# A mixture-of-experts block on one Trainium2 core: the router stage splits x itself, and the norm's weight is applied when gathered rows leave PSUM

## The chip, the cores and the metric

The kernel runs on one core of a Trainium2 chip. Its time is the device time of one execution in microseconds (us). Three executions of the kernel before took 1015.25, 1016.13 and 1021.9 us; the median is 1016.13 us. Engines are named as in the profile: PE (TensorE; PEld is its weight load), DVE (VectorE), ACT (ScalarE), POOL (GpSimd) and SP, which here only issues DMAs.

## What is computed

Two transformer blocks run on 256 tokens of width 1024. The change lies in the last third of the first block, the mixture of experts. After the memory attention `x` is updated by a projection with `w_o_mem`, and then:

```
h   = x * rsqrt(mean(x*x) + eps) * norm_ffn          # rms_norm
pg  = softmax(h @ w_rg + b_rg);  group = argmax(pg)
pe  = softmax((h @ w_re + b_re)[group]);  two best of 8 experts
y   = sum over both: weight * ((silu(h @ w_gate[e]) * (h @ w_up[e])) @ w_down[e])
x   = x + y
```

There are 32 experts, each with three matrices of 1024 x 512 float32 (6 MB), and all of them are read from HBM. A second block follows (attention and a squared-relu MLP).

## The kernel before, in words

**Stages.** `first_mixers` ends with the memory attention. `moe` then adds the projection `w_o_mem` to `x` in two halves of 512 columns (chunks `c` and `last`), routes the tokens (class `Router`), gathers each expert's tokens into slots of 64 rows, runs 16 pairs of experts (`pair(p)`), and scatters the results back into four PSUM accumulators. `second` follows.

**Two parts.** Where float32 exactness matters, an operand is split in a high part (rounded to fp32r by ACT) and a low part (the difference, by DVE or POOL), and both are multiplied. The gather uses that: `hh` and `hl` (`R.h`) are the high and low part of the normed tokens, and a one-hot matrix `D` of each group of four experts selects rows by matmul (line 1043: 4 matmuls for each of 8 slices of 128 features, 32 for a group `q` of four experts, 8 groups). The result leaves PSUM at lines 1047 (DVE) and 1049 (ACT), 512 columns at a time, into `XG[q]`.

**The router stage** (lines 1110 to 1161) is written out by hand: the order of the calls is the order of the instructions on PE, ACT, DVE and POOL. For each half of the tokens (`tb` 0 and 1):

- `project`, `add` (line 1089): `x` gets its last columns, and ACT sums the squares (line 233).
- `transposed` (785 to 790) and `logits` (795): `x`, not normed, is transposed and multiplied by the router's weights, into which `gains` (779) has put the norm's weight.
- `rms` (243 and 69 to 87, nine small DVE instructions) gives the token's factor `r`.
- `gained` (1095): POOL writes `y = x * gain`, a scaled copy of `x`, in the feature order of the gather. It lives in one of the two `raw2` buffers; the weight's rows fill one of the two `gb` buffers.
- The two parts: for `tb` 0 ACT makes `hh = y * r` (1123) and DVE `hl` (1124); for `tb` 1 ACT scales `y` (1142), rounds it to `hh` (1143), and POOL subtracts (1144).
- `groups` (800 to 805) scales the logits and finds the best group.

After both halves come `experts` (815 to 831, DVE), `counts` (838 to 840, PE), `slots`, `one_hots` (1025, 1026), `gather(0)` and then the first pair's matmuls (1062). `keep_warm` (1100) issues products of the identity that nobody reads; `init` (1104) puts `x` into the accumulators, after which x's own buffer is free for weights.

**Weights.** `feed` (991) issues the experts' loads on SP's queue, 1 MB each, in the order of use. A load goes to the next place of the list `HOMES` (r: six `raw` buffers, w: the split buffers `whi` and `wlo`, h, g: the two `gb` buffers, 2: `raw2`, x: the buffer of `x`), and only if that place is counted free in `space`; `freed` hands a place back. SP's own order is set by a scheduler, in which a load is put where its buffer is expected to come free; SP issues in that order and waits at each for the buffer's last reader.

Of the kernel before, what the change touches and what calls it, by code (L numbers as in the profile page):

```python
# [9 lines left out]
F32 = mybir.dt.float32  # L10
# [4 lines left out]
AF = mybir.ActivationFunctionType  # L15
OP = mybir.AluOpType
# [152 lines left out]
def tok(tb):  # L169
    return slice(tb * 128, tb * 128 + 128)  # L170


def half(n):
    return slice(n * 512, n * 512 + 512)
# [42 lines left out]
def load_gain(k, name, queue=None):  # L217
    gb = k.pa.tile([128, 1024], F32, name="gb", bufs=2)
    src = k.I[name]
    (queue or k.nc.gpsimd).dma_start(gb, bcast_rows(src, 1024))  # L220
    return gb
# [15 lines left out]
def rms(k, parts):  # L237

    v = small(k, 1, "rv")
    if len(parts) == 1:  # L240
        k.nc.vector.tensor_scalar(v, parts[0], RMS_EPS, None, op0=OP.add)
    else:
        k.nc.vector.tensor_scalar(v, parts[0], parts[1], RMS_EPS, op0=OP.add, op1=OP.add)
    return rsqrt(k, v, 1)
# [691 lines left out]
def moe(k, oT):  # L936
# [4 lines left out]
    x = k.x  # L941
    wg, wu, wd = I["w_gate"][0], I["w_up"][0], I["w_down"][0]
    R = Routing()
    with ExitStack() as ctx:
# [6 lines left out]
        R.flag = mp.tile([1, 1], I32, name="flag")  # L951
        R.raw2 = ctx.enter_context(tc.tile_pool(name="raw2", bufs=RAW2))

        y = R.raw2.tile([128, 2048], F32, name="raw").rearrange("p (t n) -> p t n", t=2)
        route_tables(k, R)
        gain = load_gain(k, "norm_ffn")
        w_o = I["w_o_mem"][0]
        parts = [[], []]
        c = Chunk(k, cols(w_o, 0))
# [18 lines left out]
        order = [(p, kind, h, i) for p in range(NP) for kind in range(3) for h in range(2) for i in range(2)]  # L978
        homes = cycle(HOMES)
        space = {kind: HOMES.count(kind) for kind in HOMES}  # L980
        for kind in "w2xg":
            space[kind] -= SPL if kind == "w" else 1
        weights, ahead = {}, []

# [24 lines left out]
        def freed(kind, n=1):  # L1009
            space[kind] += n  # L1010
            feed()
# [22 lines left out]
        def gather(q, parts):  # L1034

            if q not in XG:
                XG[q] = gathered_tiles(q)
            for j in parts:
                ps = k.wk.tile([128, 2, 256], F32, name="wk")
                for r in range(2):  # L1040
                    terms = [(h, tb) for h in R.h for tb in range(2)]
                    for i, (h, tb) in enumerate(terms):
                        nc.tensor.matmul(ps[:, r], h[:, tb, tok(2 * j + r)], DD[q][:, tb],
                                         start=(i == 0), stop=(i == 3))
                dst = XG[q][j // 2][:, j % 2 * 2:j % 2 * 2 + 2].rearrange("p a e s -> p a (e s)")
                if j % 2:
                    nc.vector.tensor_copy(dst, ps)
                else:
                    nc.scalar.activation(dst, ps, AF.Copy)

        def side(i):

# [36 lines left out]
            nc.vector.tensor_add(xs, xs, acc[tb])  # L1089
            parts[tb].append(mean_sq(k, xs, mp.tile([128, 512], F32, name="usb", bufs=1)))  # L1090

        def gained(tb, n):
            out = y[:, tb].rearrange("t (kt p) -> t p kt", kt=8)[:, n * 64:n * 64 + 64]
            xs, gs = (v[:, half(n)].rearrange("t (p kt) -> t p kt", kt=8) for v in (x[:, tb], gain))
            nc.gpsimd.tensor_tensor(out, xs, gs, op=OP.mult)

        def keep_warm(tb, n):

# [9 lines left out]
        macc = [[], []]  # L1108
        pool = nc.gpsimd
        with tc.manual_schedule(engines=order_of):  # L1110
            gained(0, 0)
            gained(1, 0)
            project(0, UNITS)
            q.transposed(0, 0, nc.scalar)
            add(0)
            gained(0, 1)
            q.transposed(1, 0, nc.vector)
            feed()
            project(1, UNITS[:4])
            q.transposed(0, 1, nc.scalar)  # L1120
            r0 = rms(k, parts[0])
            q.gains()
            nc.scalar.activation(hh[:, 0], y[:, 0], AF.Copy, scale=r0)
            nc.vector.scalar_tensor_tensor(hl[:, 0], y[:, 0], r0, hh[:, 0].bitcast(F32),
                                           op0=OP.mult, op1=OP.subtract)
            project(1, UNITS[4:])
            macc[0].extend(k.acc.tile([128, 512], F32, name="acc") for _ in range(2))
            freed("w", SPL)
            q.logits(0, 0)
            add(1)  # L1130
            q.transposed(1, 1, nc.scalar)
            gained(1, 1)
            freed("g")
            r1 = rms(k, parts[1])
            keep_warm(0, 2)
            q.logits(0, 1)
            keep_warm(0, 2)
            q.logits(1, 0)
            q.groups(0, r0)
            keep_warm(0, 2)  # L1140
            q.logits(1, 1)
            nc.scalar.activation(y[:, 1], y[:, 1], AF.Copy, scale=r1)
            nc.scalar.activation(hh[:, 1], y[:, 1], AF.Copy)
            pool.tensor_tensor(hl[:, 1], y[:, 1], hh[:, 1].bitcast(F32), op=OP.subtract)
            freed("2")
            q.groups(1, r1)
            init(0)
            macc[1].extend(k.acc.tile([128, 512], F32, name="acc") for _ in range(2))
            q.experts()
            keep_warm(1, 3)  # L1150
            q.counts()
            init(1)
            freed("x")
            q.slots()
            one_hots(0)
            q.exps()
            gather(0, (0, 1))
            q.slots_by_group()
            gather(0, (2, 3))
            q.rows()  # L1160
            one_hots(1)
# [147 lines left out]
def spill(k, R, macc):  # L1309

    nc, tc, I = k.nc, k.tc, k.I
    n_over = nc.values_load(R.flag[0:1, 0:1], min_val=0, max_val=512)
    with tc.If(n_over > 0):
        hT = k.pa.tile([128, 8, 256], F32, name="hTl0", bufs=1)
        for kt in range(8):
            ps = k.wk.tile([128, 256], F32, name="wk")
            h = R.mp.tile([128, 2, 128], F32, name="usb", bufs=1)
            nc.vector.tensor_add(h, *(t[:, :, tok(kt)].bitcast(F32) for t in R.h))
            for tb in range(2):
                nc.tensor.transpose(ps[:, tok(tb)], h[:, tb], k.ident)  # L1320
            nc.scalar.activation(hT[:, kt], ps, AF.Copy)
        with tc.For_i(0, NE, 1) as e:

            def half_load(name, j):
                w = R.raw2.tile([128, 2048], F32, name="raw")
                src = I[name][0][ds(e, 1)].rearrange("o (p a) n -> p (o a) n", p=128)
                a, n = src.shape[1:]
                nc.sync.dma_start(w.rearrange("p (a n) -> p a n", n=n), src[:, j * a // 2:(j + 1) * a // 2])
                return w

            pg = [[k.wk.tile([128, 512], F32, name="wk") for _ in range(2)] for _ in range(2)]
            for i, name in enumerate(("w_gate", "w_up")):
                for j in range(2):
                    w = half_load(name, j)
                    for kt in range(4):
                        for tb in range(2):
                            nc.tensor.matmul(pg[tb][i], hT[:, 4 * j + kt, tok(tb)], w[:, half(kt)],
                                             start=(j == 0 and kt == 0), stop=(j == 1 and kt == 3))
            aT = []
            at = [R.mp.tile([128, 4, 128], F32, name=name, bufs=1) for name in ("sg", "v")]  # L1340
            for tb in range(2):
                a = R.mp.tile([128, 512], F32, name=("usb", "gsb")[tb], bufs=1)
                nc.scalar.activation(a, pg[tb][0], AF.Silu)
                nc.vector.tensor_mul(a, a, pg[tb][1])
                pt = k.wk.tile([128, 4, 128], F32, name="wk")
                for f in range(4):
                    nc.tensor.transpose(pt[:, f], a[:, f:512:4], k.ident)
                t = at[tb]
                nc.scalar.activation(t, pt, AF.Copy)
                aT.append(t)  # L1350
            py = [[k.wk.tile([128, 512], F32, name="wk") for _ in range(2)] for _ in range(2)]
            for j in range(2):
                w = half_load("w_down", j)
                for f in range(2):
                    for tb in range(2):
                        for n in range(2):
                            nc.tensor.matmul(py[tb][n], aT[tb][:, 2 * j + f], w[:, half(2 * f + n)],
                                             start=(j == 0 and f == 0), stop=(j == 1 and f == 1))
            for tb in range(2):
                for n in range(2):  # L1360
                    ys = R.mp.tile([128, 512], F32, name=("usb", "gsb")[n], bufs=1)
                    nc.vector.tensor_scalar(ys, py[tb][n], R.wov[:, tb, ds(e, 1)], None, op0=OP.mult)
                    nc.tensor.matmul(macc[tb][n], k.ident, ys, start=False, stop=True,
                                     skip_group_check=True)
# [320 lines left out]
```

## Time and profile before

| | before |
|---|---|
| median of three executions | 1016.13 us (1015.25 to 1021.9) |
| profiled execution | 1020.27 us, span 1018.5 us |
| PE busy | 946.6 us (93%) |
| DVE, ACT, POOL busy | 445.7, 330.2, 137.5 us |
| HBM read | 291.28 MB, 287 GB/s over the span |
| mean granted clock of PE | 0.981 |

Times of rows are microseconds from the start of the span. In the table by stretch a busy time is a sum within the stretch, and PEclk is the share of the full clock that was granted (1.00 is 2.4 GHz, 0.50 is 1.2 GHz). In a timeline a row can stand for several instructions (xN); its length is from the first one's start to the last one's end, and square brackets hold the engine's idle time before it and what ended it.

### The profile page before, as it was taken

To read this page: it belongs to the slowest core of one execution; us is meant where nothing else is said; L and a number is where in the kernel's file an instruction comes from. 1 tells how busy PE (TensorE), PEld (TensorE's weight loads), DVE (VectorE), ACT (ScalarE), POOL (GpSimd) and SP (SyncE) were. 2 spreads that over 40 slices of the span, in tenths; PEclk is the share of its full clock that TensorE was granted. 3 is DMA by queue.
4 is the path that set the end of the run, shared out by engine and by line. 5 is a ranking of instruction groups with operands and counts; after the bars stand their busy time and mean duration, and the time that the engine had idled before them with its cause. 6 is when DMAs were issued, how large, how long until landed. Compare 5 with 4: busy or idle time off the path is not lost. (4 is left out here: it accounts for less than half of the span.)

```text
span 1018.5 us, 13363 instructions
## 1 busy us (share of the span) xinstructions
PE 946.6 (93%) x5308; PEld 658.4 (65%) x5308; DVE 445.7 (44%) x810; ACT 330.2 (32%) x518; POOL 137.5 (13%) x83
## 2 busy tenths in 40 slices
PE   9989999998999999999989999878898979999996
PEld 8969889884344444444434444325888859999995
DVE  6896875644221211121111211106845578444554
ACT  6647554531110111011111101105553436444541
POOL 1231121230000000000000000002313332211220
PEclk9989999999999999999999999998998989999999
DMA  9953553597999999999999999999534435556501
GB/s 356 351 167 133 176 186 125 176 348 268 401 425 421 424 423 422 425 422 424 422 420 423 421 421 425 423 424 352 197 125 125 155 115 169 203 189 189 201 1 42
DMA packets 85712, 293.23 MB, mean 288 GB/s; under 512 B 6992, under 2 KB 15728, under 8 KB 72080
## 3 DMA queue, kind: packets, MB, share of 16 engines
q1 hardware_dynamic: 84752, 289.56, 73.4%
q0 software_dynamic: 896, 2.79, 0.8%
q8 instruction: 43, 0.70, 0.3%
q14 instruction: 21, 0.17, 0.1%
HBM read 291.28 MB, written 1.05 MB: 287 GB/s over the span
## 5 line engine op out<-in xcount | busy, mean ns | idle before, releaser
L131 ACT ACTIVATE whi<-raw 128x1024 fp32r<-128x1024 f32 x156 | 162.9, 1058 | 149.6 <-PE acc L182 60.5
L140 DVE TENSOR_TENSOR wlo<-raw,whi 128x1024 fp32r<-128x1024 f32 x114 | 142.9, 1263 | 105.1 <-ACT whi L131 102.9
L140 POOL TENSOR_TENSOR wlo<-raw,whi 128x1024 fp32r<-128x1024 f32 x42 | 103.0, 2456 | 333.7 <-ACT whi L131 331.2
L180 PE MATMUL acc<-hTh,whi 128*128 128x256 f32 x352 | 102.3, 291 | 0.0
L182 PE MATMUL acc<-hTh,wlo 128*128 128x256 f32 x352 | 101.1, 287 | 0.3 <-DVE wlo L140 0.3
L181 PE MATMUL acc<-hTl,whi 128*128 128x256 f32 x352 | 100.8, 286 | 0.0
L1221 DVE COPY usb<-wk 128x512 f32<-128x512 f32 x16 | 11.0, 690 | 203.3 <-PE wk L1062 185.2
L1062 PE MATMUL wk<-raw,hTh 128*64 128x512 f32 x312 | 88.5, 600 | 10.5 <-DMA raw<-in_w_up 5.0
L1185 PE MATMUL wk<-raw,v 128*64 128x512 f32 x232 | 71.1, 595 | 10.8 <-issue 8.5
L1196 ACT ACTIVATE hTl<-wk,wc 128x512 fp32r<-128x512 f32 x32 | 22.0, 688 | 165.3 <-PE wk L1185 165.3
L180 PEld LDWEIGHTS acc<-hTh,whi 128*128 128x128 f32 x352 | 68.7, 195 | 1.3 <-issue 1.0
L182 PEld LDWEIGHTS acc<-hTh,wlo 128*128 128x128 f32 x352 | 68.5, 195 | 0.5 <-DVE wlo L140 0.5
L181 PEld LDWEIGHTS acc<-hTl,whi 128*128 128x128 f32 x352 | 68.6, 195 | 0.2
L1062 PE MATMUL wk<-raw,hTl 128*64 128x512 f32 x208 | 67.4, 594 | 0.0
L1062 PEld LDWEIGHTS wk<-raw,hTh 128*64 128x64 f32 x312 | 28.3, 138 | 58.5 <-issue 42.3
L181 PE MATMUL acc<-wlo,hTh 128*128 128x512 f32 x160 | 63.8, 399 | 1.7 <-DVE wlo L140 1.7
L1197 DVE SCALAR_TENSOR_TENSOR hTl<-wk,wc,hTl 128x512 fp32r<-128x512 f32 x32 | 24.0, 751 | 91.7 <-ACT hTl L1196 89.9
L180 PE MATMUL acc<-whi,hTh 128*128 128x512 f32 x160 | 63.6, 398 | 0.0
L180 PE MATMUL wk<-hTh,whi 128*128 128x256 f32 x224 | 63.5, 284 | 0.0
L182 PE MATMUL acc<-whi,hTl 128*128 128x512 f32 x160 | 63.5, 398 | 0.0
L182 PE MATMUL wk<-hTh,wlo 128*128 128x256 f32 x224 | 63.4, 283 | 0.0
L181 PE MATMUL wk<-hTl,whi 128*128 128x256 f32 x224 | 63.4, 283 | 0.0
(409 smaller groups left out, 1775.8 us busy)
## 6 DMA issues: line engine op xcount, KB each, us to landing
raw<-in_w_up SPq DMA_DIRECT2D x49, 1024.0 KB, 11.0
raw<-in_w_down SPq DMA_DIRECT2D x45, 1024.0 KB, 11.1
raw<-in_w_gate SPq DMA_DIRECT2D x32, 1024.0 KB, 14.1
whi<-in_w_down SPq DMA_DIRECT2D x25, 512.0 KB, 11.1
wlo<-in_w_down SPq DMA_DIRECT2D x25, 512.0 KB, 9.9
whi<-in_w_up SPq DMA_DIRECT2D x20, 512.0 KB, 12.0
wlo<-in_w_up SPq DMA_DIRECT2D x20, 512.0 KB, 11.4
whi<-in_w_gate SPq DMA_DIRECT2D x19, 512.0 KB, 10.5
```

Source lines behind the costliest of these rows:

```text
L131: self.k.nc.scalar.activation(hi, self.quarter(len(self.his)), AF.Copy)
L140: eng.tensor_tensor(lo, self.quarter(i), self.his[i].bitcast(F32), op=OP.subtract)
L180: nc.tensor.matmul(out, lh, rh, start=start, stop=False, skip_group_check=True)
L181: nc.tensor.matmul(out, lh, rl, start=False, stop=False, skip_group_check=True)
L182: nc.tensor.matmul(out, ll, rh, start=False, stop=stop, skip_group_check=True)
L1062: nc.tensor.matmul(ps[side(i)], xg[:, 2 * (p % 2) + i], w[:, half(kt % 2)], start=(kt == 0), stop=(kt == 7), tile_position=(0, 64 * i), sk ...
L1185: nc.tensor.matmul(py[n][side(i)], v[:, f, side(i)], w[:, half(n)], start=(f == 0), stop=(f == 3), tile_position=(0, 64 * i), skip_group_c ...
L1196: nc.scalar.activation(yh[:, s], py[n], AF.Copy, scale=R.wc[:, p:p + 1])
L1197: nc.vector.scalar_tensor_tensor(yl[:, s], py[n], R.wc[:, p:p + 1], yh[:, s].bitcast(F32), op0=OP.mult, op1=OP.subtract)
L1221: nc.vector.tensor_copy(u, ps)
```

## The change

The scaled copy `y` goes. Both parts are made from `x` itself, for both halves of the tokens with one ACT and one DVE instruction (`normed`), so POOL has no arithmetic left in the stage. The parts lie in x's feature order, so the gather's stationary operand now takes every eighth column (`2 * j + r:1024:8`). The norm's weight, as a table `R.gain` of 8 columns, is multiplied in where a gathered slice leaves PSUM: 256 columns at a time, the even slice by ACT and the odd one by DVE. The six idle products between the logits go; three ahead of `counts` stay. `groups(0)` moves ahead of `rms` of the second half, and the places `2` and `g` are counted free from the start.

```diff
--- before.py
+++ after.py
@@ -951,9 +951,9 @@
         R.flag = mp.tile([1, 1], I32, name="flag")
         R.raw2 = ctx.enter_context(tc.tile_pool(name="raw2", bufs=RAW2))
 
-        y = R.raw2.tile([128, 2048], F32, name="raw").rearrange("p (t n) -> p t n", t=2)
         route_tables(k, R)
-        gain = load_gain(k, "norm_ffn")
+        R.gain = mp.tile([128, 8], F32, name="gain")
+        nc.gpsimd.dma_start(R.gain, I["norm_ffn"].rearrange("o (p kt) -> p (o kt)", kt=8))
         w_o = I["w_o_mem"][0]
         parts = [[], []]
         c = Chunk(k, cols(w_o, 0))
@@ -978,7 +978,7 @@
         order = [(p, kind, h, i) for p in range(NP) for kind in range(3) for h in range(2) for i in range(2)]
         homes = cycle(HOMES)
         space = {kind: HOMES.count(kind) for kind in HOMES}
-        for kind in "w2xg":
+        for kind in "wx":
             space[kind] -= SPL if kind == "w" else 1
         weights, ahead = {}, []
 
@@ -1040,13 +1040,15 @@
                 for r in range(2):
                     terms = [(h, tb) for h in R.h for tb in range(2)]
                     for i, (h, tb) in enumerate(terms):
-                        nc.tensor.matmul(ps[:, r], h[:, tb, tok(2 * j + r)], DD[q][:, tb],
+                        nc.tensor.matmul(ps[:, r], h[:, tb, 2 * j + r:1024:8], DD[q][:, tb],
                                          start=(i == 0), stop=(i == 3))
-                dst = XG[q][j // 2][:, j % 2 * 2:j % 2 * 2 + 2].rearrange("p a e s -> p a (e s)")
-                if j % 2:
-                    nc.vector.tensor_copy(dst, ps)
-                else:
-                    nc.scalar.activation(dst, ps, AF.Copy)
+                for r in range(2):
+                    kt = 2 * j + r
+                    dst = XG[q][j // 2][:, kt % 4].rearrange("p e s -> p (e s)")
+                    if r:
+                        nc.vector.tensor_scalar(dst, ps[:, r], R.gain[:, kt:kt + 1], None, op0=OP.mult)
+                    else:
+                        nc.scalar.activation(dst, ps[:, r], AF.Copy, scale=R.gain[:, kt:kt + 1])
 
         def side(i):
 
@@ -1089,10 +1091,11 @@
             nc.vector.tensor_add(xs, xs, acc[tb])
             parts[tb].append(mean_sq(k, xs, mp.tile([128, 512], F32, name="usb", bufs=1)))
 
-        def gained(tb, n):
-            out = y[:, tb].rearrange("t (kt p) -> t p kt", kt=8)[:, n * 64:n * 64 + 64]
-            xs, gs = (v[:, half(n)].rearrange("t (p kt) -> t p kt", kt=8) for v in (x[:, tb], gain))
-            nc.gpsimd.tensor_tensor(out, xs, gs, op=OP.mult)
+        def normed(tb, r):
+
+            nc.scalar.activation(hh[:, tb], x[:, tb], AF.Copy, scale=r)
+            nc.vector.scalar_tensor_tensor(hl[:, tb], x[:, tb], r, hh[:, tb].bitcast(F32),
+                                           op0=OP.mult, op1=OP.subtract)
 
         def keep_warm(tb, n):
 
@@ -1108,41 +1111,28 @@
         macc = [[], []]
         pool = nc.gpsimd
         with tc.manual_schedule(engines=order_of):
-            gained(0, 0)
-            gained(1, 0)
             project(0, UNITS)
             q.transposed(0, 0, nc.scalar)
             add(0)
-            gained(0, 1)
             q.transposed(1, 0, nc.vector)
             feed()
             project(1, UNITS[:4])
             q.transposed(0, 1, nc.scalar)
             r0 = rms(k, parts[0])
             q.gains()
-            nc.scalar.activation(hh[:, 0], y[:, 0], AF.Copy, scale=r0)
-            nc.vector.scalar_tensor_tensor(hl[:, 0], y[:, 0], r0, hh[:, 0].bitcast(F32),
-                                           op0=OP.mult, op1=OP.subtract)
+            normed(0, r0)
             project(1, UNITS[4:])
             macc[0].extend(k.acc.tile([128, 512], F32, name="acc") for _ in range(2))
             freed("w", SPL)
             q.logits(0, 0)
             add(1)
             q.transposed(1, 1, nc.scalar)
-            gained(1, 1)
-            freed("g")
-            r1 = rms(k, parts[1])
-            keep_warm(0, 2)
             q.logits(0, 1)
-            keep_warm(0, 2)
             q.logits(1, 0)
             q.groups(0, r0)
-            keep_warm(0, 2)
+            r1 = rms(k, parts[1])
             q.logits(1, 1)
-            nc.scalar.activation(y[:, 1], y[:, 1], AF.Copy, scale=r1)
-            nc.scalar.activation(hh[:, 1], y[:, 1], AF.Copy)
-            pool.tensor_tensor(hl[:, 1], y[:, 1], hh[:, 1].bitcast(F32), op=OP.subtract)
-            freed("2")
+            normed(1, r1)
             q.groups(1, r1)
             init(0)
             macc[1].extend(k.acc.tile([128, 512], F32, name="acc") for _ in range(2))
@@ -1315,10 +1305,10 @@
         for kt in range(8):
             ps = k.wk.tile([128, 256], F32, name="wk")
             h = R.mp.tile([128, 2, 128], F32, name="usb", bufs=1)
-            nc.vector.tensor_add(h, *(t[:, :, tok(kt)].bitcast(F32) for t in R.h))
+            nc.vector.tensor_add(h, *(t[:, :, kt:1024:8].bitcast(F32) for t in R.h))
             for tb in range(2):
                 nc.tensor.transpose(ps[:, tok(tb)], h[:, tb], k.ident)
-            nc.scalar.activation(hT[:, kt], ps, AF.Copy)
+            nc.scalar.activation(hT[:, kt], ps, AF.Copy, scale=R.gain[:, kt:kt + 1])
         with tc.For_i(0, NE, 1) as e:
 
             def half_load(name, j):
```

On PE, in the router stage from the first half's logits to the counts (`lp` is the tile of the logits, `ident` the identity, `M` the one-hot of the chosen experts), the one piece of the difference reads:

```order
-L795 MATMUL wk<-wr,hTl_2345 128x36 x4
 L785 MATMUL wk<-ident,x 128x128 x4
-L1100 MATMUL acc<-ident 128x128 x2
-L795 MATMUL wk<-wr,hTl_2345 128x36 x4
-L1104 MATMUL acc<-x,ident 128x512 x2
+L795 MATMUL wk<-wr,hTl_2344 128x36 x12
+L1107 MATMUL acc<-x,ident 128x512 x2
+L1103 MATMUL acc<-ident 128x128 x3
 L838 LDWEIGHTS tri
```

Of the rows that repeat, two more pairs of idle products and two more groups of four logits' products are left out here. Afterwards twelve products of the logits follow one another, then `init(0)` and the three idle products, as before.

On DVE, from the second half's add on, the kernel before has (`gp` and `lg` are the scaled logits; the row L87 ends `rms`):

```order
L1089 TENSOR_TENSOR x<-x,acc 128x512
L243 TENSOR_SCALAR rv<-ms 128x1
L87 TENSOR_SCALAR rqr<-rqt,rqx,rqi 128x1
L800 SCALAR_TENSOR_TENSOR gp<-wk,rqr,rb 128x4
L805 MAX_INDEX gi_2350<-g_2349,gp 128x8
L815 TENSOR_TENSOR g_2572<-iof,gi_2350 128x8
L817 TENSOR_TENSOR ep<-lg,g_2572 128x64
```

and the changed kernel, in the same place (of `rms` the first and the last row, of `groups` the first of each):

```order
L1091 TENSOR_TENSOR x<-x,acc 128x512
L805 MAX_INDEX gi_2349<-g_2348,gp 128x8
L243 TENSOR_SCALAR rv<-ms 128x1
L87 TENSOR_SCALAR rqr<-rqt,rqx,rqi 128x1
L1097 SCALAR_TENSOR_TENSOR hl<-x,rqr,big_2355 128x1024
L802 SCALAR_TENSOR_TENSOR lg<-wk,rqr,rb 128x32
L815 TENSOR_TENSOR g_2560<-iof,gi_2349 128x8
L817 TENSOR_TENSOR ep<-lg,g_2560 128x64
```

`groups(0)` has moved from behind `rms` to ahead of it, and the low part of the second half, POOL's before, stands between `rms` and `groups(1)`.

On SP, at the loads of chunk `last` (`in_w_o_mem`) and the first experts', the difference begins:

```order
-L116 DMA raw<-in_w_o_mem 128x4x512 x4
-L1005 DMA raw<-in_w_gate 128x2048 x2
-L1005 DMA raw<-in_w_up 128x2048
+L116 DMA raw<-in_w_o_mem 128x4x512 x2
 L1005 DMA gb<-in_w_gate 128x1024
```

The first of the two half-size loads to the `gb` buffers now stands ahead of the last two loads of `w_o_mem`. Further on, the second of them and a 1 MB load to `raw2` have moved from behind the loads to `whi` and `wlo` to ahead of them.

## Rows read from the trace of the kernel before

**Rows 1.** Busy table by stretch: length, busy us (count) by engine, clock, DMA share, GB/s

```profile
230.00:237.00 7.00, 4.34 (x17) 1.98 (x16) 6.10 (x27) 0.00 (x0) 2.20 (x1) 1.00 0.86 324
242.00:246.00 4.00, 4.00 (x20) 1.29 (x18) 2.33 (x6) 0.00 (x0) 0.00 (x0) 1.00 0.02 4
300.00:690.00 390.00, 360.64 (x1736) 162.90 (x1734) 64.89 (x114) 41.81 (x66) 2.34 (x1) 1.00 1.02 423
```

**Rows 2.** Timeline of SP's queue, 205 to 262: start, length, instruction

```profile
236.60 0.33 SPq L1005 DMA_DIRECT2D x<-in_w_up  x1
245.47 0.80 SPq L1005 DMA_DIRECT2D raw<-in_w_up  x2
```

**Rows 3.** Timeline of PE, 215 to 262: start, length, instruction [idle before]

```profile
225.37 0.61 PE L1100 MATMUL acc<-ident 128*128 128x128 f32 x4
225.82 0.98 PE L795 MATMUL wk<-wr,hTl 128*128 128x36 f32 x8
...
234.53 0.18 PE L838 MATMUL wk<-M,tri 128*128 128x32 bf16 x1 [2.58 <-DVE M L831]
...
234.60 1.96 PE L1104 MATMUL acc<-x,ident 128*128 128x512 f32 x4
...
237.47 0.36 PE L1043 MATMUL wk<-D,big 128*128 128x256 f32 x1 [0.55 <-DVE d L864]
```

**Rows 4.** Timeline of DVE, 205 to 262

```profile
222.94 1.28 DVE L1124 SCALAR_TENSOR_TENSOR hl<-raw,rqr,big 128x1024 fp32r<-128x1024 f32 x1 [2.00 <-ACT big L1123]
224.15 0.68 DVE L1089 TENSOR_TENSOR x<-x,acc 128x512 f32<-128x512 f32 x1
225.67 0.21 DVE L243 TENSOR_SCALAR rv<-ms 128x1 f32<-128x1 f32 x1 [0.85 <-ACT usb L233]
...
227.31 0.21 DVE L800 SCALAR_TENSOR_TENSOR gp<-wk,rqr,rb 128x4 f32<-128x4 f32 x1
...
229.52 0.22 DVE L800 SCALAR_TENSOR_TENSOR gp<-wk,rqr,rb 128x4 f32<-128x4 f32 x1 [1.49 <-PE wk L795]
...
230.28 1.95 DVE L815 TENSOR_TENSOR g<-iof,gi 128x8 f32<-128x8 f32 x1
232.26 0.22 DVE L817 TENSOR_TENSOR ep<-lg,g 128x64 f32<-128x64 f32 x1
```

**Rows 5.** Timeline of ACT, 205 to 262

```profile
221.76 1.14 ACT L1123 ACTIVATE big<-raw,rqr 128x1024 fp32r<-128x1024 f32 x1
...
227.48 1.15 ACT L1142 ACTIVATE raw<-raw,rqr 128x1024 f32<-128x1024 f32 x1 [1.31 <-DVE rqr L87]
```

**Rows 6.** Timeline of POOL, 180 to 262

```profile
229.86 2.34 POOL L1144 TENSOR_TENSOR hl<-raw,big 128x1024 fp32r<-128x1024 f32 x1 [3.67 <-ACT big L1143]
```

**Rows 7.** Weight loads by line: ns min/median/max, first and last start, form

```profile
L785 PEld LDWEIGHTS wk<-ident,x x16: 138/140/143, 216.8 to 225.2; 128*128 128x128 f32 x16
...
L1043 PEld LDWEIGHTS wk<-D,big x128: 186/188/202, 236.5 to 622.5; 128*128 128x128 f32 x128
...
L1168 PEld LDWEIGHTS wk<-ident,gsb x64: 195/212/220, 257.0 to 681.7; 128*128 128x128 f32 x64
```

**Rows 8.** Timeline of PE, two places where it resumes after a gap

```profile
519.85 1.09 PE L1062 MATMUL wk<-raw,hTh 128*64 128x512 f32 x1 [2.81 <-DVEq L1313]
...
831.23 1.08 PE L1506 MATMUL wk<-ident,a 128*128 128x128 f32 x4 [3.43 <-DVE a L1499]
```

**Rows 9.** Busy table of the stretches in which the clock came back there

```profile
522.00:524.00 2.00, 2.00 (x10) 0.67 (x8) 0.00 (x0) 0.00 (x0) 0.00 (x0) 0.80 1.03 416
836.00:838.00 2.00, 2.00 (x9) 1.59 (x8) 0.82 (x2) 0.00 (x0) 0.00 (x0) 0.80 0.02 4
```

**Rows 10.** Costliest groups: count, busy us, mean ns, idle before and its releasers

```profile
L1062 PE MATMUL wk<-raw,hTh 128*64 128x512 f32 x312 | 88.5, 600 | 10.5 <-DMA raw<-in_w_up 5.0 <-DVEq L1313 2.8 <-DMA raw<-in_w_gate 2.7
```

**Rows 11.** The same view for two copies out of PSUM on DVE

```profile
L1047 DVE COPY hTh<-wk 128x512 f32<-128x512 f32 x8 | 5.5, 692 | 23.5 <-PE wk L1043 23.5
...
L366 DVE TENSOR_TENSOR t<-wk,t 128x256 fp32r<-128x256 f32 x8 | 3.0, 418 | 0.8 <-ACT t L365 0.8
```

## The prediction

> **What bounds the kernel now.** I read the busy table by stretch first. From 300 to 690 us the DMA engines are busy without a break (share 1.02) at 423 GB/s, while PE computes 360.64 of 390 us [rows 1]: the sixteen pairs of experts run at the speed at which weights arrive. The only line of PE in there that waits for data is 1062, with 5.0 + 2.7 = 7.7 us put down to weight loads in the whole run [rows 10]; that is PE's spare time in the loop. So work added or saved inside the loop counts only beyond that.
>
> Second, where does this stream start? From 242 to 246 the DMA share is 0.02 [rows 1]. SP's queue tells why: the load into x's buffer is issued at 236.60, and the next one only at 245.47, when the first pair has used up its first weights [rows 2]. All buffers are full and the stream stands still until PE computes. The amount loaded by then is fixed by the buffers, so **the end moves with the start of the first pair**, one for one, and loading earlier gains nothing.
>
> Third, what sets that start: the chain through the router stage. PE waits 2.58 us for DVE's row 831 before the counts, and 0.55 us for the one-hots [rows 3]. DVE is busy for 6.10 of the 7.00 us from 230 on [rows 1]. The reader should see in DVE's timeline that the comparison of 128x8 numbers at line 815, begun at 230.28, takes 1.95 us, though line 817, with 64 columns, takes 0.22; it ends when POOL's subtraction ends, 229.86 + 2.34 = 232.20 [rows 4, 6]. POOL's work holds DVE up there, on the path.
>
> **The change part by part.** All times are of the profiled execution (1020.27 us with a span of 1018.5; the median of the runs shown, 1016.13, is 4.1 lower); I add the sum to the median.
>
> *DVE's chain.* Up to the second add (224.15) nothing on it moves: `hh` of the first half waited for ACT's copy, not for `y`. Now `groups(0)` comes next and needs the logits of the first half. PE starts them where the first idle products stood, 225.37, and eight records last 0.98: 226.35 [rows 3]. A dependent instruction follows 0.04 after its source (1123 ends at 222.90, 1124 starts at 222.94) [rows 4, 5], so 226.39. `groups` takes 230.28 - 229.52 = 0.76: 227.15. `rms` takes 227.48 - 225.67 = 1.81 until ACT can start on its result [rows 4, 5]: 228.96. ACT's `hh` takes 1.14 as line 1123: 230.10. DVE's `hl` starts 0.04 later and the next instruction 224.15 - 222.94 = 1.21 after that [rows 4, 5]: 231.35. `groups(1)` 0.76: line 815 starts at 232.11. No POOL instruction is left to hold it up, so it takes about as long as line 817, 0.22 [rows 4]; line 817 starts at 232.33, against 232.26 before. **Sum: +0.07 us.** The 1.73 us that the stall gives back are spent on `hl`, which now stands in DVE's line.
>
> *The gather's weight loads.* The stationary operand is read with a step of eight floats. The trace has no such load. Below: a load of 188 ns that hides behind a matmul costs nothing, +0. Above: the transposes with a step of four floats (1168) load in 212 ns, those without a step (785) in 140 [rows 7]; if 72 ns more show in full, 32 loads cost 2.3 us on the path. A gain is excluded, since the same numbers are read from more places. PE overlaps a load with the matmul before, so I take a value nearer to the row of hidden loads: 0.02 each, **+0.7 us**. In the loop there are seven more groups, 224 of the 256 loads [rows 7]: 224 x 0.02 = 4.5 us, under the 7.7 that PE has to spare, so nothing.
>
> A rule that speaks against this change: the Trainium skill, "SBUF — State Buffer", section "Door 1: The DMA port swizzle (why `[64,N]` ≈ `[32,N]`)", says that SBUF is read in lines of 16 bytes, and that an access pattern pays when successive elements fall on different lines, so that float32 may be read with a step of up to four free of charge. Here every element falls on a line of its own. The trace differs for the step of four, which is not free in it; the page gives no price, so by the rule the term of 0.7 is some positive number, and by the row it is bounded by 2.3.
>
> *The idle products.* Three blocks go, each moving what follows by about 225.82 - 225.37 = 0.45 [rows 3], 1.4 in all. PE, which ended at 234.53 - 2.58 = 231.95, ends at about 230.6 and stays idle until 234.60: 4.0 us. They are work for nothing only while the clock stays up. Before, the gap of 2.58 us left it at 1.00 [rows 1, 3]. But after gaps of 2.81 and 3.43 us PE resumed with matmuls of 1.09 and 1.08 us [rows 8], and the clock was at 0.80 in the mean of 522 to 524 and of 836 to 838 [rows 9]. With two levels, 1.2 and 2.4 GHz, a mean of 0.80 over 2 us is 0.8 us at the lower, so it came back at 522.8 and 836.8: 2.9 and 5.6 us after work had resumed. I expect the same here. `init(1)` takes 0.45 a record at full clock (1.96 for four, the last 0.6 of which overlaps) [rows 3], 0.9 at half. If the clock returns 2.9 us after 234.65, three records are done at half speed and the last follows at full: the gather goes on at 237.9 rather than 237.54 (237.47 + 0.07), +0.35. If after 5.6 us, `init(1)` ends at 238.25 and the gather runs 2 us at half: 0.7 + 1.0 = +1.7. I take the middle, **+1.0 us**.
>
> *Copies out of PSUM.* A slice of 256 columns takes DVE 0.42 against 0.69 for 512 [rows 11]. There are twice as many, but ACT and DVE share each tile. Cover: the first pair's first weights need slices 0 to 3, and PE is still gathering slices 4 to 7 then. If the cover went, one copy, 0.4 us, would show. In the loop it is hidden with all else.
>
> *DMAs.* The 512 KB of weight rows become a table of 4 KB, issued last on POOL's queue, well ahead of the gather. Loads to `gb` and `raw2`, 2 MB in all, are issued earlier. One of them now stands ahead of `last`'s chunk on SP's queue. Its buffer's reader is long done; what it costs the chunk is 0.5 MB at 423 GB/s [rows 1], 1.2 us of a wait that the memory attention covers. On the other side nothing is gained, since the stream stands still at 242 either way. x's load follows `init(1)`; it moves by 1.7 us at most, towards a stretch in which the stream stands still for 4.
>
> Sum: 0.07 + 0.7 + 1.0 = **+1.8 us**, 1017.9 us (1022.1 for an execution like the profiled one).
>
> **The rivals.**
>
> *Slower: strided loads bind PE.* If each load shows 72 ns, the path takes 2.3 us, and the loop 224 x 0.072 = 16.1, of which 7.7 are spare and 8.4 are not. With the clock's 1.0 and 0.07 that is +11.8: 1027.9 us. It decides from 7.7 / 224 = 34 ns a load on. For it: line 1168's 212 ns. Against it: PE pulls loads ahead of matmuls of 256 columns, and in the gather before 188 ns stay hidden behind them. Chance 0.08; twice that price (1050) 0.01.
>
> *The clock stays up*, as after the gap of 2.58 us, since three idle products still stand close to the gap: +0.8, 1016.9 us. Chance 0.25.
>
> *The stall stays.* If line 815 is slow for a reason of its own and not for POOL's, `hl` is added and nothing given back: 1.8 + 1.73 = +3.5, 1019.6 us. For it: it is the only instruction of its kind. Against it: its end agrees with POOL's to 0.03 us. Chance 0.08.
>
> *Faster: the loop is bound by PE.* Then the half copy ahead of `v` (0.69 - 0.42 = 0.27 us in each of 14 pairs) would count: -3.8, with the sum 1014.1 us. Against it: DMA share 1.02. Chance 0.06.
>
> **How the numbers follow.** My forecast has a chance of 0.52, with bounds 0.07 + 0.35 + 0 = +0.4 and 0.07 + 1.7 + 2.3 = +4.1, so 1016.5 to 1020.2. Three executions of one kernel spread over 6.6 us, and a median can lie a microsecond or two lower on another day; to take in the PE-bound case and the stall that stays, the range goes from 1014 to 1022. What it leaves out is mostly the strided case. A measurement tells some 1% (10 us) from no change, and only the strided loads reach that: faster 0.01, same 0.90, slower 0.09.
>
> **What would show it.** In the changed kernel's profile the comparison (815) should take about 0.2 us and line 817 start 232.33 - 224.15 = 8.2 us after the second add; `hl` of the second half should stand in front of it with 1.28 us. The granted clock should fall below 1.00 between 230 and 240. The gather's loads should last between 188 and 260 ns, and its matmuls start at most 0.03 us further apart than before. The DMA share should be near zero just ahead of the first pair's second half, for longer than before, and 1.02 from there on. I am wrong if the loop's share falls below 1, if the gather's matmuls start 0.07 us further apart than before, or if the first pair starts more than 4 us later or more than 1 us earlier, counted from the second add.

## The result and the profile after

The changed kernel takes 1062.97 us (median of four executions, 1061.44 to 1068.18), the kernel before 1016.88 beside it (1015.25 to 1021.9): a ratio of 1.0433, with a 95% interval of 1.0403 to 1.0463. It is **46 us slower**; the prediction was 1017.9, in 1014 to 1022. The profiled execution has a span of 1059.4 us against 1018.5, and a mean granted clock of 0.964 against 0.981.

The busy table by stretch, after (length, then busy us and count of PE, PEld, DVE, ACT, POOL, then clock, DMA share, GB/s):

```profile
230.00:237.00 7.00, 3.23 (x14) 1.94 (x13) 5.08 (x29) 1.01 (x1) 0.00 (x0) 0.86 0.59 240
242.00:246.00 4.00, 4.00 (x18) 4.00 (x18) 1.14 (x4) 0.95 (x2) 0.00 (x0) 1.00 0.27 115
300.00:690.00 390.00, 365.50 (x1584) 174.71 (x1586) 67.24 (x126) 43.62 (x74) 0.00 (x0) 0.95 0.97 394
```

Against [rows 1] the loop's DMA share has fallen from 1.02 to 0.97 and its clock from 1.00 to 0.95, and in the same 390 us PE gets through 1584 matmuls where it did 1736. The weights no longer set the pace. From 242 to 246 PEld, the weight load, is busy all of the 4.00 us. The gather's line, by form, says why (ns min/median/max, first and last start):

```profile
L1043 PEld LDWEIGHTS wk<-D,big x128: 312/338/343, 238.3 to 675.4; 128*128 128x128 f32 x128
L1043 PE MATMUL wk<-D,big x128: 397/407/738, 238.3 to 675.6; 128*128 128x256 f32 x128
```

A load with the step of eight floats lasts 338 ns, not 188 [rows 7] (the other half of the loads, those of `hl`, have the same median). The timelines of PE, DVE and ACT show the router stage and one of the waits in the loop (start, length; in brackets the idle time before, and what ended it):

```profile
235.48 0.19 PE L838 MATMUL wk<-M,tri 128*128 128x32 bf16 x1 [3.77 <-DVE M L831]
235.56 3.39 PE L1107 MATMUL acc<-x,ident 128*128 128x512 f32 x4
239.14 0.65 PE L1043 MATMUL wk<-D,hl 128*128 128x256 f32 x2
239.63 0.65 PE L1043 MATMUL wk<-D,big 128*128 128x256 f32 x2
240.11 0.65 PE L1043 MATMUL wk<-D,hl 128*128 128x256 f32 x2
246.93 3.65 PE L1064 MATMUL wk<-raw,hTl 128*64 128x512 f32 x16
...
328.39 0.65 PE L1043 MATMUL wk<-D,hl 128*128 128x256 f32 x2
330.76 1.09 PE L1175 MATMUL wk<-raw,v 128*64 128x512 f32 x1 [1.72 <-issue]
```

```profile
225.25 0.68 DVE L1091 TENSOR_TENSOR x<-x,acc 128x512 f32<-128x512 f32 x1
231.05 1.28 DVE L1097 SCALAR_TENSOR_TENSOR hl<-x,rqr,big 128x1024 fp32r<-128x1024 f32 x1 [1.22 <-ACT big L1096]
233.00 0.17 DVE L815 TENSOR_TENSOR g<-iof,gi 128x8 f32<-128x8 f32 x1
233.21 0.22 DVE L817 TENSOR_TENSOR ep<-lg,g 128x64 f32<-128x64 f32 x1
...
329.58 0.48 DVE L1049 TENSOR_SCALAR hTl<-wk,gain 128x256 f32<-128x256 f32 x1 [4.73 <-ACT hTl L1051]
329.98 0.68 DVE L1217 TENSOR_TENSOR v<-sg,wk 128x512 f32<-128x512 f32 x1
```

```profile
329.07 0.47 ACT L1051 ACTIVATE hTl<-wk,gain 128x256 f32<-128x256 f32 x1 [3.62 <-PE wk L1043]
```

Three things follow from these rows.

First, four of the gather's matmuls start in 0.97 us (239.14 to 240.11): one every 0.242. In the run with neighbouring columns below it is 0.12. That is 32 x 0.121 = 3.9 us in front of the first pair, which starts 246.93 - 225.25 = 21.68 behind the second add. Before, it was 241.79 - 224.15 = 17.64 [rows 4], by this row:

```profile
241.79 3.65 PE L1062 MATMUL wk<-raw,hTl 128*64 128x512 f32 x16
```

In the loop it is 224 x 0.121 = 27.1 us of PE time.

Second, `v`. ACT's copy of the gathered tile ends at 329.54, and only then does DVE start its own copy of the other half (329.58). The product that makes `v` is behind it, and the down projection waits 1.72 us. The waits of PE for `v` over the loop, after, from 258 to 735 (us in all, times, longest):

```profile
PE wk L1175 <- issue: 22.4, 13, 1.7
PE wk L1175 <- DVE v L1217: 3.4, 3, 1.7
```

Before, from 258 to 690, the first of these was about 1.43 us each time, as the next row shows; the second was 4.5 us in 4 times.

```profile
PE wk L1185 <- issue: 17.2, 12, 1.5
```

Third, the clock. Two stretches of 2 us from 330 on (PE's busy time and count, clock, DMA share, GB/s):

```profile
330.00:332.00 2.00, 1.24 (x4) 0.65 1.02 416
332.00:334.00 2.00, 2.00 (x6) 0.50 1.03 422
```

PE resumes at the lower of its two levels, 1.2 GHz; its first matmul takes 1.09 us instead of 0.59. An estimate of what the clock costs over the span is (1 - mean clock) x span: before 0.019 x 1018.5 = 19.4 us, after 0.036 x 1059.4 = 38.1, so 18.7 more. It is an upper estimate, since it also counts time at the lower clock in which PE stood idle.

Now it is SP that waits for PE. Its longest waits from 258 to 735 (us, times, longest); before, from 258 to 690, the two largest of this kind were 22.8 and 11.9 us:

```profile
SPq L1005 <- PE wk L1175: 164.5, 43, 13.6
SPq L1005 <- PE wk L1064: 136.6, 68, 12.4
```

### The profile page after: what moved, and what is told of

It reads as the page before. It is cut to its first block, busy times and chain, and to the rows that moved or that the text cites. A ratio compares the mean times of both kernels' runs of the same rounds, so it can differ in the third digit from the quotient of the medians.

```text
span 1059.4 us, 13366 instructions
## 1 busy us (share of the span) xinstructions
PE 991.0 (94%) x5296; PEld 689.9 (65%) x5296; DVE 449.8 (42%) x827; ACT 334.7 (32%) x533; POOL 130.1 (12%) x78
## 5 line engine op out<-in xcount | busy, mean ns | idle before, releaser
L1175 PE MATMUL wk<-raw,v 128*64 128x512 f32 x232 | 83.6, 677 | 12.9 <-issue 12.1
L1064 PE MATMUL wk<-raw,hTh 128*64 128x512 f32 x312 | 86.0, 598 | 2.8 <-SPq L1303 2.8
L1243 POOL TENSOR_TENSOR gb<-gb 128x1024 f32<-128x1024 f32 x1 | 2.4, 2355 | 487.6 <-DMA gb<-in_norm_mix_pre 487.6
L1175 PEld LDWEIGHTS wk<-raw,v 128*64 128x64 f32 x232 | 25.8, 155 | 50.3 <-issue 49.3
```

The costliest lines, as they stand in the source:

```text
L1064: nc.tensor.matmul(ps[side(i)], xg[:, 2 * (p % 2) + i], w[:, half(kt % 2)], start=(kt == 0), stop=(kt == 7), tile_position=(0, 64 * i), sk ...
L1175: nc.tensor.matmul(py[n][side(i)], v[:, f, side(i)], w[:, half(n)], start=(f == 0), stop=(f == 3), tile_position=(0, 64 * i), skip_group_c ...
```

## The experiments

Each run stands beside executions of the kernel before that were taken with it (medians 1018.5 to 1020.24 us); how much of the 46 us is gone in a run, or still there, is counted from that median. In the code, `...` stands for lines left out.

**Theory L**: the strided weight loads cost 0.12 us each; the longer waits for `v` and the lower clock come behind them. **Rival C**: the two copies, ACT and DVE on one tile, are the cause. **Rival K**: it is the clock, which falls because the idle products are gone.

**Neighbouring columns.** The changed kernel with one line of the gather undone:

```
-  nc.tensor.matmul(ps[:, r], h[:, tb, 2 * j + r:1024:8], DD[q][:, tb],
+  nc.tensor.matmul(ps[:, r], h[:, tb, tok(2 * j + r)], DD[q][:, tb],
```

> The changed kernel, with the gather's stationary operand read as 128 neighbouring columns again; the gathered features are then in another order than the weights expect, so this run is for its time only. Theory L (the weight load with a step of eight floats costs all of it, by itself and through the clock that falls behind it in the loop): line 1043's loads are back at 188 ns, its matmuls start every 0.12 us instead of 0.24, the DMA share from 300 us on is 1.02 again, and the time is about 1017 us (1015 to 1019). Rival C (the copies out of PSUM, split in two instructions on two engines, or the idle products that went, cost a good part): the time stays above 1030 us.

Measured: 1019.5 us, half a microsecond above the range expected, and level with the kernel before beside it: a ratio of 1.0002 (0.9982 to 1.0023). Without the step nothing of the 46 us is left. Its loads, its gather and its loop:

```profile
L1043 PEld LDWEIGHTS wk<-D,big x128: 186/188/243, 238.2 to 628.3; 128*128 128x128 f32 x128
```

```profile
238.26 0.81 PE L1043 MATMUL wk<-D,big 128*128 128x256 f32 x2
...
239.39 0.40 PE L1043 MATMUL wk<-D,hl 128*128 128x256 f32 x2
239.62 0.41 PE L1043 MATMUL wk<-D,big 128*128 128x256 f32 x2
239.87 0.40 PE L1043 MATMUL wk<-D,hl 128*128 128x256 f32 x2
...
243.03 3.65 PE L1064 MATMUL wk<-raw,hTl 128*64 128x512 f32 x16
...
291.76 7.09 PE L1175 MATMUL wk<-raw,v 128*64 128x512 f32 x32 [1.72 <-issue]
```

```profile
300.00:690.00 390.00, 359.64 (x1740) 163.73 (x1738) 68.53 (x127) 46.03 (x78) 2.34 (x1) 1.00 1.02 423
```

Two starts per 0.24 us now. The wait of 1.72 for `v` is there too, since the copies are still shared, but behind it PE runs 32 matmuls in 7.09 us, at full clock. So the wait alone brings neither the low clock nor the loss, and rival C falls as a cause by itself. The idle products are missing in this run too, and the loop's clock is 1.00: that already speaks against rival K.

**The kernel before with the step.** POOL writes `y` in the order of `x`, and the gather takes the step:

```
-  nc.tensor.matmul(ps[:, r], h[:, tb, tok(2 * j + r)], DD[q][:, tb],
+  nc.tensor.matmul(ps[:, r], h[:, tb, 2 * j + r:1024:8], DD[q][:, tb],
...
-  out = y[:, tb].rearrange("t (kt p) -> t p kt", kt=8)[:, n * 64:n * 64 + 64]
...
+  nc.gpsimd.tensor_tensor(y[:, tb, half(n)], x[:, tb, half(n)], gain[:, half(n)], op=OP.mult)
```

> The kernel before, with nothing changed but the order of the features in the scaled copy: POOL writes it in x's order, and the gather reads its stationary operand with a step of eight. Copies, idle products and the order of the loads are those of before. Theory L: loads of 338 ns, matmuls every 0.24 us, 4 us more ahead of the first pair, 27 us more in the loop and some 20 us lost to the lower clock, less 8 to spare: 1055 to 1063 us. Rival C: 1017 us plus the 31 us of the loads less 8 to spare at most, under 1042 us, since the single copy of before leaves the wait for v as it was.

Measured: 1053.17 us, ratio 1.0335 (1.0303 to 1.0368), two below the bottom of what was expected. The step costs 33 us with nothing else of the change: the idle products, single copies and POOL work are in place. The rest up to 46 needs the change's other parts. The loop:

```profile
300.00:690.00 390.00, 370.03 (x1616) 176.53 (x1614) 61.06 (x107) 40.00 (x63) 0.00 (x0) 0.95 0.98 398
```

Its clock is 0.95 as in the changed kernel, though no idle product is gone and PE's waits for `v` are the 1.42 us of before. So the low clock in the loop comes with the dear loads, not with the missing idle products nor with the longer waits.

**A clock kept up.** Seven idle products ahead of the down projection's matmuls:

```
+  for i in range(7):
+      nc.tensor.matmul(py[0][:, 0:128], k.ident, k.ident, start=True, stop=True)
```

> The changed kernel, with seven idle products of the identity ahead of each pair's last matmuls (line 1175), where PE waits 1.7 us for v. They are issued ahead of the wait and fill it. Theory L says that of the 46 us some 20 are matmuls at half clock behind that wait: the granted clock stays at 1.00 in the loop, line 1175 is back at 595 ns, and the time falls to 1043 us (1040 to 1047). Rival: the lower clock has time to hide in and the loop is held by something else (the loads of weights, the copies): the clock is back, but the time stays above 1055 us.

Measured: 1042.15 us, ratio 1.0222 (1.0189 to 1.0255). The loop:

```profile
300.00:690.00 390.00, 385.77 (x1846) 189.86 (x1844) 68.08 (x127) 44.77 (x76) 2.35 (x1) 1.00 1.00 412
```

The clock is back at 1.00 and about 24 of the 46 us with it; what is lost to the clock is 0.020 x 1044.0 = 20.9, about as before. PE now fills 385.77 of 390 us, idle products included, and the kernel is still 22 us slow. The clock carries about half of the loss and is not its beginning: with the two runs above, rival K falls.

**One copy.** Each gathered tile is copied by one engine as before, without the norm's weight:

```
+  if j % 2:
+      nc.vector.tensor_copy(dst, ps)
+  else:
+      nc.scalar.activation(dst, ps, AF.Copy)
```

> The changed kernel with the copies out of PSUM as before: 512 columns by one engine, ACT for even and DVE for odd slice pairs. The norm's weight is left out in it, so its result lacks that factor. In the changed kernel DVE's copy starts only behind ACT's of the same tile, so v comes 0.3 us later than before. Theory: this is what lies between the changed kernel (1063) and the kernel before with the step alone (1053): PE's wait for v is 1.4 us again, the clock falls behind fewer of them, and the time is 1051 to 1056 us. Rival: the order of the router stage or the loads' order makes the difference, and the time stays at 1060 to 1065 us.

Measured: 1054.57 us, ratio 1.0363 (1.0322 to 1.0404). PE waits 1.42 us for `v` again, and about 10 of the 46 us go; what is left, 36, is near the 33 of the step alone.

**`v` first.** The step stays; the second pair of copies is issued behind the product that makes `v`:

```
-  gather(nxt, todo[1:])
+  late = gather(nxt, todo[1:], True)
   ...
   nc.vector.tensor_mul(v, sg, pt)
+  if late:
+      copied(nxt, *late)
```

> The changed kernel, step of eight kept, with one move: of the second slice pair that each expert pair gathers, the two copies out of PSUM come behind the product v instead of ahead of it. PE's gather products then cover the wait for v. If the loss in the loop is PE's time (27 us of loads, 5 us of longer waits, some 19 us at half clock behind those waits), the waits and the lower clock go with this move although no load gets faster: the clock is 1.00 in the loop and the time falls to 1020 to 1028 us, set by the transfers again. Rival: the loads alone bind the loop, and only the clock's part comes back: 1040 to 1045 us.

Measured: 1024.64 us, ratio 1.0063 (1.0033 to 1.0093). The loop, and all that is left of the wait for `v`:

```profile
300.00:690.00 390.00, 382.68 (x1742) 176.41 (x1738) 69.54 (x126) 47.41 (x80) 2.37 (x1) 1.00 1.02 423
```

```profile
PE wk L1181 <- DVE v L1223: 1.7, 2, 0.8
```

This is the run that explains the size. The loads are as dear as in the changed kernel (median 338 ns), PE does 382.68 us of work in 390, and yet the weights set the pace again (1.02). That is 23.0 us more than with neighbouring columns (359.64), for as many matmuls; six of the gather's groups lie in this stretch, and 192 x 0.121 is 23.2. Of the 46 us 40 are gone, though no load became cheaper; most of the 6 that stay go with the first pair, which starts at 246.62, 4.8 us later than before. The dear loads fit into the loop when PE does not also stand idle some 26 us for `v` (22.4 + 3.4 above); it is the two together that overfill it, and with the low clock that comes with them they make the 46.

**Other steps.** In one kernel the eight groups of the gather read with steps 1 to 8:

> A measurement of the disputed cost by itself: the changed kernel, in which group q (0 to 7) of the gather reads its stationary operand with a step of q + 1 floats, so steps 1 to 8 stand in one trace; the gathered features are wrong in all groups but the last, and the run is for the durations of line 1043 only. If an element on a line of its own is what costs, the load is at 188 ns for a step of 1, longer for 2 and 3, and the same for all steps from 4 to 8 (338). If the distance itself costs, it rises with every step up to 338 at eight. If eight (32 bytes) is a special case, steps 5 to 7 are as cheap as 4, where the transposes took 212 ns.

Loads of line 1043 with steps 1, 2, 3, 4 and 8, and starts of its matmuls with steps 2 and 3:

```profile
L1043 PEld LDWEIGHTS wk<-D,big x16: 186/188/193, 237.7 to 241.9; 128*128 128x128 f32 x16
...
L1043 PEld LDWEIGHTS wk<-D,big x8: 193/198/208, 249.9 to 261.4; 128*128 128x128 f32 x8
...
L1043 PEld LDWEIGHTS wk<-D,big x8: 253/262/268, 305.6 to 317.9; 128*128 128x128 f32 x8
...
L1043 PEld LDWEIGHTS wk<-D,big x16: 308/332/334, 366.5 to 410.9; 128*128 128x128 f32 x16
...
L1043 PEld LDWEIGHTS wk<-D,big x16: 312/338/342, 615.4 to 660.0; 128*128 128x128 f32 x16
```

```profile
250.27 0.40 PE L1043 MATMUL wk<-D,hl 128*128 128x256 f32 x2
...
250.75 0.40 PE L1043 MATMUL wk<-D,hl 128*128 128x256 f32 x2
...
306.08 0.52 PE L1043 MATMUL wk<-D,hl 128*128 128x256 f32 x2
...
306.78 0.52 PE L1043 MATMUL wk<-D,hl 128*128 128x256 f32 x2
```

Steps 5 to 7 have medians of 318, 322 and 328. The price rises up to a step of four floats, 16 bytes, and stays about there. The spacing of the matmuls tells how much of a load is hidden: with step 2 (198 ns) four start in 0.48 us, one every 0.12 as without a step; with step 3 (262 ns) four in 0.70, one every 0.175.

**Permuted parts.** ACT and DVE write both parts in the gather's order, so that its loads read neighbouring columns (the last transposes likewise):

```
+  by = ("p kt", "kt p")[tb]
+  hi, lo = (t[:, tb].rearrange("t (kt p) -> t " + by, kt=8) for t in R.h)
+  xs = x[:, tb].rearrange("t (p kt) -> t " + by, kt=8)
```

> The changed kernel, but both parts are written in the gather's order (feature 8p + kt at column 128kt + p), so the gather reads neighbouring columns and all results are right. For the first half of the tokens ACT and DVE read x in a row and write with a step of 128 floats, for the second they read x with a step of eight and write in a row: the trace of one run prices both. Theory L: the loads are at 188 ns and the time is that of the kernel before, 1017 to 1020 us, provided that the four instructions of the parts stay near 1.14 and 1.28 us; a step that doubles one of them for the second half adds its surplus to the chain, 1 us each. Rival: moving the step from PE to ACT and DVE only moves the cost, each of the four instructions takes 3 us or more, and the first pair starts 4 us later or more.

Measured: 1024.41 us, ratio 1.0052 (1.0028 to 1.0076), 4 us above the 1020 expected (2 with the 1 us allowed for each instruction slowed in the second half), though the loop is bound by weights again. The step has moved into ACT's and DVE's instructions, on the path:

```profile
224.99 2.24 DVE L1100 SCALAR_TENSOR_TENSOR hl<-x,rqr,big 128x1024 fp32r<-128x1024 f32 x1 [2.95 <-ACT big L1099]
...
234.96 2.07 DVE L1100 SCALAR_TENSOR_TENSOR hl<-x,rqr,big 128x1024 fp32r<-128x1024 f32 x1 [2.22 <-ACT big L1099]
```

```profile
232.78 2.15 ACT L1099 ACTIVATE big<-x,rqr 128x1024 fp32r<-128x1024 f32 x1 [3.33 <-DVE rqr L87]
```

Each takes 0.8 to 1.0 us more than without a step (1.28 and 1.14, [rows 4, 5]); the 3 us of the rival are not reached, but its later start of the first pair is: 247.41, 5.6 us later than before. The clock has a part in it. The second add stands behind the longer `hl` of the first half, PE waits 2.00 us for it and resumes at the lower level (0.50 granted from 230 to 237). The 24 logit records take 5.17 us instead of the 2.77 of the changed kernel, and DVE waits 2.58 us for the first of them, 1.57 in the changed kernel:

```profile
228.61 5.17 PE L795 MATMUL wk<-wr,hTl 128*128 128x36 f32 x24
```

**Both remedies**, permuted parts and `v` first, with the idle products between the logits back:

> The changed kernel with the two remedies together: both parts are written in the gather's order, so that its loads read neighbouring columns (as in the run with permuted parts), and the second pair of copies of a gathered tile comes behind v's product (as in the run with v first); the idle products between the logits are back. Theory L (the loop's loss is the price of strided loads, with waits for v and the low clock behind it): the loop is again bound by the weight loads (DMA share 1.02, clock 1.00), so what is left is the 4 to 6 us by which the permuted parts, with their step in ACT's and DVE's instructions, put the first pair later; the clock's loss falls from 22.5 us (permuted parts) to 16 to 19: 1019 to 1023 us, level with the kernel before or up to 0.5% slower. Rival (the copies on two engines, or the missing POOL work, cost something of their own that neither remedy removes): 1024 us or more, as either remedy alone, with a DMA share below 1.02 in the loop.

Measured: 1025.83 us, ratio 1.0051 (1.0034 to 1.0068): above the 1019 to 1023 expected, and in the range of the rival. But the loop is as theory L has it (share 1.02, clock 0.99), and the rival wanted a share below 1.02, so it does not explain the miss. The clock's loss is 0.027 x 1023.3 = 27.6 us, where 16 to 19 was expected. The router stage shows why:

```profile
227.56 1.12 PE L785 MATMUL wk<-ident,x 128*128 128x128 f32 x4 [2.00 <-DVE x L1097]
...
229.32 1.76 PE L795 MATMUL wk<-wr,hTl 128*128 128x36 f32 x8
230.88 1.20 PE L1111 MATMUL acc<-ident 128*128 128x128 f32 x4
...
248.21 3.65 PE L1070 MATMUL wk<-raw,hTl 128*64 128x512 f32 x16
```

As with the permuted parts alone, PE waits for the second add, which stands behind the longer `hl`, and resumes at half clock (0.50 granted from 230 to 237): eight logit records take 1.76 us, not the 0.98 of [rows 3]. The idle products stand between the logits that DVE waits for, at 1.20 us a block instead of 0.61, and the first pair starts later still, 6.4 us later than before, which is about what the run lost (5.6). In both runs the end moves with the start of the first pair, as the prediction said. None of the versions tried is faster than the kernel before.

## Why the prediction was wrong

**The step that failed** is "The gather's weight loads": 0.02 us each, "nearer to the row of hidden loads". It is 0.12, six times that, and 1.7 times the upper bound of 72 ns. The bound was the difference between two kinds of transposes, 212 ns with a step of four (line 1168) and 140 without (785). The gather's loads take 188 without a step and 332 with four, 144 ns more, so neither row was like the load in question. Nor was there cover left: loads of 188 and 198 ns leave 0.12 us between two matmuls, one of 262 ns 0.175, one of 338 ns 0.242, so nearly all that a load lasts beyond some 200 ns shows. On the path that is 3.9 us, for which 0.7 was written; in the loop 27.1, for which 4.5 was written and then nothing counted. All three signs of being wrong that the prediction named came true: a share below 1 (0.97), matmuls more than 0.07 us further apart (0.12), and a first pair more than 4 us later (21.68 - 17.64 = 4.04).

The Trainium skill, "SBUF — State Buffer", section "Door 1: The DMA port swizzle (why `[64,N]` ≈ `[32,N]`)", was the page that spoke against the change, and the steps of one to eight fit its lines of 16 bytes: beyond four floats no further price (318 to 338 ns). What it says of float32 up to a step of four, that it is free, the runs contradict for these loads: 262 ns at three and 332 at four, against 188.

**The spare time.** "7.7 that PE has to spare" was near enough for the changed kernel as it is ordered: by the prediction's own sum with 0.121 us a load, 27.1 - 7.7 = 19.4 in the loop and 3.9 on the path would have been forecast, 23 us (24.4 with its 1.0 and 0.07), and the run with the clock kept up is 22 us slow. But 7.7 holds only the waits for data. PE's idle time in the loop is 390 - 360.64 = 29 us [rows 1], most of it waits for `v` (17.2 + 4.5 us from 258 to 690). The `v`-first run shows that these could be filled, the changed kernel that they were not.

**The second failure** is the clock. It was forecast to fall in the router stage and was not looked for in the loop, where it fell from 1.00 to 0.95; most of the 18.7 us lie there. Why it falls there was not found; the runs show only that it comes with the dear loads. And `v` was forecast 0.27 us *earlier* because its half copy is shorter; it came 0.3 later, because the two halves of one tile are copied one after the other (0.47 + 0.48 against 0.69). What makes DVE wait for ACT there is not shown.

The sum with measured sizes: path 3.9, loop 27.1 - 7.7, clock 18.7, 13 waits for `v` at 0.3 us = 3.9: 45.9 us, against 46.1 between the medians. But the clocks and waits are those of the profiled executions, and between these it is 40.9, so the sum is 5 us too high, and the upper estimate for the clock may be why. The parts are not independent either, as the `v`-first run shows, so the sum is a rough consistency, not a decomposition. The rival "strided loads bind PE" named the right mechanism and the right place where it decides, 34 ns a load. Its time (1027.9) was short because its price of 72 ns was; with 121 it would have been 1016.1 + 24.4 = 1040.5, which still lacks the clock and the waits in the loop. Its chance of 0.08 was too small for a price that the trace of before did not hold. The "1050" at twice the price is a slip: the same sum gives 30.2 us, 1046 on the median; 1050 comes of adding it to the profiled execution's 1020.27.

**What was right.** Line 815 takes 0.17 us without POOL beside it, and line 817 starts 233.21 - 225.25 = 7.96 us after the second add (forecast 8.2, before 8.11). PE's gap ahead of the counts is 3.77 us (forecast 4.0), and the clock falls to 0.86 from 230 to 237, with `init(1)` at 3.39 us instead of 1.96. But the 1.0 us set down for it was too much: in the run with neighbouring columns the first pair starts 243.03 - 225.19 = 17.84 behind the second add, before 17.64, so 0.2. Its gather starts at 238.26, 13.07 behind the add; before, the gather's second record started 237.47 - 224.15 = 13.32 behind it, having waited 0.55 for the one-hots [rows 3]. What `init(1)` loses is mostly taken up by that wait. DVE's copies of 256 columns take 0.48 us (forecast 0.42). The moved DMAs cost nothing that the run with neighbouring columns shows, as forecast.

## What to carry to other kernels

An operand whose step is new to the trace has no price in it: bound it from above by what the engine would do if nothing of it were hidden, and give that case a chance that fits what is not known. Removing a copy that also put numbers in order moves that order into a reader; count how often the reader runs (here 256 loads, for four instructions on POOL). And a stage that is bound by transfers has room for PE work only if PE's own waits leave it: look at its busy time in the stage and at every wait, and ask what the clock does behind each.

## What the runs showed of the hardware that was not expected

A stationary load of 128x128 float32 in the gather lasts 188, 198, 262, 332 and 338 ns at steps of 1, 2, 3, 4 and 8 floats, and its matmuls of 256 columns start every 0.12, 0.12, 0.175, 0.23 and 0.242 us. A step of two is nearly free; eight is hardly dearer than four. DVE and ACT pay for a step as well: 1024 columns with a step take 2.07 to 2.24 us on DVE against 1.28, and 2.15 on ACT against 1.14. And PE's clock stayed at 1.00 behind waits of 1.72 us in the loop with quick loads, while with dear loads it fell behind most waits of the same length, and behind waits of 1.42 us in the kernel before with the step. The runs show that the two go together; why, they leave open.
